# Sum of squares for 1/rms taken from the transposed input, with its row sent through memory

## The chip, the cores and the metric

The program runs on one core of a Trainium2 chip. The metric is the device time of one execution in microseconds (us); lower is better. The core has TensorE (PE in the profile; its weight loads are PEld), VectorE (DVE), ScalarE (ACT), GpSimd (POOL) and SyncE (SP), each with its own queue of instructions, and 16 DMA engines that move data between the chip's memory and the core's own memory. TensorE writes into PSUM banks; the other engines read them from there, except GpSimd, whose operands here are all in SBUF.

## The reference

The input is 512 tokens of 1024 features in FP32. One Mamba-2 layer comes first, then one projection to shared keys and values, then one layer of differential attention, and a last RMSNorm. The change lies in the first norm and the first product:

```
h = rms_norm(x, norm_g)          # y = x * rsqrt(mean(x*x, axis=-1) + EPS), then * g
zxbcdt = h @ w_in                # z (2048), x/B/C (4096), dt (32)
xbc = silu(conv(xbc)); dt = softplus(dt_raw + dt_bias)
y = ssd_chunked_scan(xs * dt, a * dt, bm, cm)   # decays exp(cumsum(a * dt))
y = gated_group_rms_norm(y + d_skip * xs, z, gate_norm_g)
x = x + y @ w_out
```

The norm's factor 1/rms is one number for each token. Since it multiplies a whole row of `h`, it can be applied after the product instead of before it.

## The kernel before

**Products.** Every FP32 operand is split into a high part (`hi`, rounded to fp32r) and the rest (`lo`), and each product is three fp32r products: hi*hi, hi*lo, lo*hi (`mm3`, `tok_mm`). The weights come in tiles of 1 MB (`raw`), in two buffers; ScalarE makes `whi` (with the norm's gain in it), VectorE `wlo`, in three buffers each. A tile serves 48 products of 512 columns. The transposed input `x_t` comes as four tiles `xt` of two feature blocks of 128 by 512 tokens; `split_x` makes `a_hi` and `a_lo` from them (named `hh` and `hl` in the code).

**The start.** TensorE first runs 17 transposes of the identity into a bank that nothing reads (`warm`). Then it runs the first half of the first z block (`pz0`: four token blocks by four feature blocks, 48 products) as the tiles come. ScalarE casts, VectorE subtracts; the two are held in program order there. The second half of z stands behind the setup of dt in the program, but it is not held there and runs ahead of it.

**1/rms.** The four token tiles `x_tok` are loaded behind the first weights; `squares` squares them on ScalarE with a sum along the features; `scales` takes the root on VectorE (`rsqrt`, a bit trick with two corrections), which gives `r_col`, 1/rms with the tokens on the partitions. For 1/rms along the free dimension on all partitions (`r_row`) GpSimd writes four diagonal blocks, TensorE multiplies a block of ones by them (`aps_r`, one FP32 product of 512 columns), and ScalarE copies the result. `r_col` scales the z block in `z_out` (Silu on ScalarE); `r_row` scales the dt rows and each x/B/C block in `conv`.

**dt and decays.** `ps_dt` is the dt product; `pre`, softplus and the running sum `acs` follow on VectorE and ScalarE. `acs` goes to memory and comes back broadcast to all partitions (`dec`) with two loads of 1 MB; its transposes (`ps_tt`, called "tt") give it by token. GpSimd subtracts and masks, ScalarE takes the exponential.

**Order.** A planner with a time simulation orders each engine's instructions; work that is ready may be put into an idle slot ahead of earlier work that is not. Where `T.on`, `A.on` or `V.on` is set, an instruction stays behind the one traced before it on its engine. From group 0 on TensorE's order is written out: `first_layer` counts one step for each three products, and `PLACES` says at which step after the end of each group's projection the parts of its scan run: "cb" the C*B product, "bt" and "xt" transposes, "st" the state products (`psA`, `psB`, `pyd`), "o1" and "o2" the outputs from the state, "y0" and "y2" the last transposes (`pyt`). "tt" is at step 22. TensorE waits where it reaches a part whose operands are late. The eight entries of a row are the groups 0 to 7.

**Queues.** Nearly all loads are issued by SP, in one order; a load that waits for a buffer holds back those behind it. The parameters `prm` go over ScalarE's queue.

Of the kernel before, what the change touches and what calls it, by code (L numbers as in the profile page):

```python
# [9 lines left out]
F32 = mybir.dt.float32  # L10
F32R = mybir.dt.float32r
I32 = mybir.dt.int32
AF = mybir.ActivationFunctionType
ALU = mybir.AluOpType
# [3 lines left out]
P = 128  # L18
S = 512
D = 1024  # L20
NT = S // P
# [17 lines left out]

PLACES = {  # L40
# [7 lines left out]
    "y2": (None,) * 7 + (72,),  # L48
}

# [28 lines left out]
def trunk(ctx, tc, x, x_t, par, w_dt, w_in, w_out, w_kvqg, w_bo, d_skip, lam_qk, fin_g, out):  # L79
# [16 lines left out]
    def ss_bank(name):  # L96
        turns[0] += 1
        tag = "mm" if turns[0] % turns[1] >= 3 else "ss"
        return psum.tile([P, 512], F32, tag=tag, name=name, bufs=3 if tag == "ss" else 4)

    def long_bank(name):
        return psum.tile([P, 512], F32, tag="long", name=name)
# [11 lines left out]
    nc.scalar.dma_start(prm[:], par[:, 0:C_CB])  # L114
    prc = const.tile([P, N_PAR - C_CB], F32, name="prc")
    x_tok = res.tile([P, NT, D], F32, name="x_tok")
    ident = const.tile([P, P], F32, name="ident")
    make_identity(nc, ident)
    sg1 = const.tile([P, 1], F32, name="sg1")
# [89 lines left out]
    def use(seg):  # L209
        fetch(segs.index(seg) + 3)  # L210
        return ready.pop(seg)
# [92 lines left out]
    def run(gen):  # L304
        for _ in gen:
            pass
# [13 lines left out]

    def squares(ss, t, sq=None):
        if sq is None:
            sq = small.tile([P, D], F32, tag="wide", name=f"sq{t}", bufs=2)
        A.activation(sq, x_tok[:, t, :], AF.Square, accum_out=ss[:, t:t + 1])

    def scales(tag, ss):

        V.tensor_scalar(out=ss, in0=ss, scalar1=ROOT2 / D, scalar2=ROOT2 * EPS, op0=ALU.mult, op1=ALU.add)  # L330
        col = const.tile([P, NT], F32, tag="r_col", name=f"{tag}r_col")
        V.tensor_copy(col, rsqrt(ss, NT, "y"))
        w = small.tile([P, NT + 1, P], F32, tag="wide", name=f"{tag}diag", bufs=2)
        GP.memset(w[:, NT], 1.0)
        for t in range(NT):
            GP.tensor_tensor(out=w[:, t], in0=ident, in1=col[:, t:t + 1].to_broadcast([P, P]), op=ALU.mult)
        ps = long_bank(f"{tag}ps_r")
        T.on = True
        T.matmul(ps, lhsT=w[:, NT], rhs=w[:, 0:NT].rearrange("p t n -> p (t n)"), start=True, stop=True)
        T.on = False  # L340
        row = res.tile([P, S], F32, tag="r_row", name=f"{tag}r_row")
        A.copy(row, ps)
        return col, row

    def turn_rows(tag, t, xn, hh, hl):

# [15 lines left out]
    def tok_mm(ps, t, b, w, ks=range(4)):  # L362
        tk = slice(t * P, (t + 1) * P)
        for k in ks:
            kk = 4 * b + k
            mm3(ps, (hh[:, kk, tk], hl[:, kk, tk]), (w[0][:, k, :], w[1][:, k, :]), b == 0 and k == 0, b == 1 and k == 3)
            yield
# [12 lines left out]
    def z_out(j, t, ps):  # L380

        for i in range(2):
            zs = bp2.tile([P, 256], F32, tag="zs", name=f"zs{j}_{t}_{i}", bufs=12)
            A.activation(zs, ps[:, i * 256:(i + 1) * 256], AF.Silu, scale=r_col[:, t:t + 1])
            zt[2 * j + i, t] = zs
# [1 line left out]


    warm = ss_bank("warm")
    for i in range(17):  # L390
        T.transpose(warm[:, 0:P], ident, ident)
    xt = [bp2.tile([P, 2, S], F32, tag="yl", name=f"xt{i}", bufs=4) for i in range(4)]

    def split_x(k, n=slice(0, S)):
        A.copy(hh[:, k, n], xt[k // 2][:, k % 2, n])
        V.tensor_tensor(out=hl[:, k, n], in0=xt[k // 2][:, k % 2, n], in1=hh[:, k, n].bitcast(F32), op=ALU.subtract)


# [4 lines left out]
    wh, wl = ready.pop(("z", 0, 0))  # L403
    pz0 = [mm_bank(f"pz0_{t}") for t in range(NT)]
    V.on = A.on = True
    for k in range(4):
        lay(first[k])
        for n in (slice(0, 256), slice(256, S)) if k < 2 else (slice(0, S),):
            split_x(k, n)
    V.on = A.on = False  # L410
    for k in range(4):
        for t in range(NT):
# [2 lines left out]
    for k in range(4, KD):  # L415
        split_x(k)
    fetch(2)
    for t in range(NT):
        nc.sync.dma_start(x_tok[:, t, :], x[t * P:(t + 1) * P, :])
    ss = bss[:, 1]  # L420
    for t in range(NT):
        squares(ss, t)
    r_col, r_row = scales("a", ss)
    V.tensor_scalar(out=sg1, in0=prm[:, C_SG:C_SG + 1], scalar1=0.5 * (1.0 - LAM0), scalar2=None, op0=ALU.mult)
    dtw_raw = sm.tile([P, KD, H], F32, name="dtw_raw")
    nc.sync.dma_start(dtw_raw[:], w_dt)
# [2 lines left out]


    V.tensor_tensor(out=dtw_raw, in0=dtw_raw, in1=prm[:, C_GA:C_GA + KD].unsqueeze(2).to_broadcast([P, KD, H]), op=ALU.mult)
    ps_dt = ss_bank("ps_dt")
    T.on = True
    for k in range(KD):
# [27 lines left out]
    A.activation(ea, prm[:, C_AL:C_AL + 1], AF.Exp)  # L462
    adt = q2
    V.tensor_scalar(out=adt, in0=dtp, scalar1=ea, scalar2=-1.0, op0=ALU.mult, op1=ALU.mult)
    ones = sm.tile([P, P], F32, name="ones")
    GP.memset(ones, 1.0)
    acs = e1
    V.tensor_tensor_scan(out=acs, data0=ones, data1=adt, initial=0.0, op0=ALU.mult, op1=ALU.add)
    acs_d = tc.dram_tile([H, NQ, P], F32, name="acs_d")
# [5 lines left out]
    nc.sync.dma_start(dsk[:], d_skip.partition_broadcast(P))  # L475


    w0 = use(("z", 0, 1))
    for t in range(NT):
        run(tok_mm(pz0[t], t, 1, w0))  # L480
        z_out(0, t, pz0[t])


    tok = const.tile([P, 4, NQ, H], F32, name="tok")
# [2 lines left out]
    def turned():  # L487
        yield "tt"
        ps_tt = ss_bank("ps_tt")
        for i, src in enumerate((dtp, acs, toe)):  # L490
            T.transpose(ps_tt[:, i * P:(i + 1) * P], src, ident)
        V.tensor_copy(tok[:, 0:3].rearrange("p a c h -> p (a c h)"), ps_tt[:, 0:3 * P])
        A.activation(tok[:, 3], tok[:, 1], AF.Exp)
        decays((0, 1))

    def runs_of(kind=1):

# [97 lines left out]
        assert not due  # L595

    decs = {}

    def decays(gs):

        for g in gs:
            hs = slice(R * g, R * g + R)
            both = bp.tile([P, N_DEC], F32, tag="dec", name=f"dec{g}", bufs=2)
            dec = both[:, 0:R * NQ * P].rearrange("p (h c l) -> p h c l", h=R, c=NQ)
            een = both[:, R * NQ * P:R * NQ * P + 2 * R].rearrange("p (h q) -> p h q", h=R)
            nc.sync.dma_start(both[:, 0:R * NQ * P],
                                acs_d[hs].rearrange("h c l -> (h c l)").partition_broadcast(P))
            GP.tensor_copy(een, dec[:, :, 1:3, P - 1])
            for h in range(R):
                GP.tensor_tensor(out=dec[:, h], in0=dec[:, h], in1=acs_tok[:, :, R * g + h].unsqueeze(2).to_broadcast([P, NQ, P]), op=ALU.subtract)  # L610
                GP.affine_select(out=dec[:, h], in_=dec[:, h], compare_op=ALU.is_ge, fill=-BIG, base=0,
                                 pattern=[[0, NQ], [1, P]], channel_multiplier=-1)
            decs[g] = (dec, een, both)

        for g in gs:
            A.activation(decs[g][2][:, 0:R * NQ * P + 2 * R], decs[g][2][:, 0:R * NQ * P + 2 * R], AF.Exp)
# [604 lines left out]
```

## Time and profile before

| | |
|---|---|
| median of 3 runs (lowest, highest) | 705.49 us (705.47, 708.14) |
| the profiled execution, whole | 707.18 us |
| its span in the profile | 705.4 us |
| mean granted TensorE clock | 0.998 |
| busy: PE, PEld, DVE, ACT, POOL | 696.1, 580.7, 524.2, 426.3, 116.1 us |
| moved by DMA | 70.85 MB |

The span runs from the first to the last instruction that the profile shows. Busy time is the time in which an engine has an instruction in work; the ends of matmuls are modelled, since they overlap, so the pace of TensorE is read from the starts of its instructions. In a row of the timeline stand the start and the length in us, the engine, the line (L70 is the helper through which VectorE, ScalarE and TensorE are called), the operation, output <- inputs, the shape, how many instructions are merged in the row, and in brackets the idle time before it and what ended it. A transpose is shown as a MATMUL, an FP32 product as two. A row of a group has the count, the busy time, the mean length in ns, and the idle time before.

### The profile page before, as it was taken

What the parts mean: (1) busy time and instruction counts of PE and PEld (TensorE: products, weight loads), DVE (VectorE), ACT (ScalarE), POOL (GpSimd) and SP (SyncE); (2) the same over time, 40 slices, a digit from 0 to 9 for tenths busy, and PEclk for the clock granted to TensorE, in tenths of its full rate; (3) what the DMA queues carried; (4) which work ended last, traced back from release to release, by engine and by line L of the source; (5) the groups of instructions that cost most, each with busy time, mean ns of one, the idle gap of its engine ahead of it and who ended that gap; (6) DMA issues with size and microseconds to landing.
All of it is one profiled execution on the core that took longest, in us unless ns stands there. A gap on an engine that the chain in (4) does not pass through costs nothing.

```text
span 705.4 us, 10468 instructions
## 1 busy us (share of the span) xinstructions
PE 696.1 (99%) x3838; PEld 580.7 (82%) x3838; DVE 524.2 (74%) x1181; ACT 426.3 (60%) x931; POOL 116.1 (16%) x158
## 2 busy tenths in 40 slices
PE   8999999999999999999999999999999999999996
PEld 7888788888878888888888888888888888888884
DVE  5499967799489679569995757557778757787776
ACT  6859663573654547536635258567777667665546
POOL 0008242502406025042110101000000000000002
PEclk9999999999999999999999999999999999999999
DMA  8654314214125323313222111513112221130103
GB/s 293 257 193 170 120 60 135 105 61 179 42 79 180 105 76 120 110 70 120 64 84 94 60 60 53 194 60 113 67 60 77 80 83 61 60 106 14 31 1 119
DMA packets 13491, 70.85 MB, mean 100 GB/s; under 512 B 1792, under 2 KB 3328, under 8 KB 6016
## 3 DMA queue, kind: packets, MB, share of 16 engines
q1 hardware_dynamic: 13008, 69.90, 27.6%
q8 instruction: 30, 0.49, 0.3%
q10 hardware_dynamic: 432, 0.28, 0.1%
q14 instruction: 21, 0.17, 0.1%
HBM read 68.02 MB, written 2.16 MB: 99 GB/s over the span
## 4 chain that ended last, share of the span: by engine, by line
PE 78%; DVE 8%; ACT 5%; DMA 4%; issue 3%; POOL 2%; SPq 0%; ACTq 0%; POOLq 0%; DVEq 0%
PE po L70 16%; PE pg L70 14%; PE pt L70 8%; PE pq L70 6%; PE pk L70 6%; PE pv L70 6%; PE pz L70 6%; PE pb L70 3%; DMA raw<-in_w_in 3%; PE sc L70 3%; DVE wlo L70 2%; ACT whi L70 2%; PE pc L70 2%; PE pyd L70 2%; DVE xc L70 1%
## 5 line engine op out<-in xcount | busy, mean ns | idle before, releaser
L70 DVE SCALAR_TENSOR_TENSOR wlo<-raw,prm,whi 128x512 fp32r<-128x512 f32 (+1 forms) x240 | 149.3, 672 | 54.0 <-ACT whi L70 53.7
L70 ACT ACTIVATE whi<-raw,prm 128x512 fp32r<-128x512 f32 (+1 forms) x240 | 133.2, 629 | 46.7 <-PE pg L70 12.0
L70 PE MATMUL pg<-a_hi,whi 128*128 128x512 f32 x256 | 102.8, 402 | 0.0
L70 PE MATMUL pg<-a_hi,wlo 128*128 128x512 f32 x256 | 99.9, 390 | 0.0
L70 PE MATMUL pg<-a_lo,whi 128*128 128x512 f32 x256 | 99.7, 389 | 0.0
L70 DVE SCALAR_TENSOR_TENSOR xc<-pg,prc,xc 128x511 f32<-128x511 f32 (+2 forms) x96 | 70.9, 743 | 12.3 <-ACT xc L70 11.2
L70 PEld LDWEIGHTS pg<-a_hi,wlo 128*128 128x128 f32 x256 | 48.1, 188 | 10.3
L70 PEld LDWEIGHTS pg<-a_hi,whi 128*128 128x128 f32 x256 | 48.2, 188 | 9.6 <-ACT zs L70 0.2
L70 PEld LDWEIGHTS pg<-a_lo,whi 128*128 128x128 f32 x256 | 48.1, 188 | 9.4
L70 PE MATMUL po<-whi,yh 128*128 128x512 f32 x128 | 51.2, 400 | 0.0
L70 PE MATMUL pz<-whi,a_hi 128*128 128x512 f32 x128 | 49.7, 397 | 0.3 <-ACT a_hi L70 0.3
L70 PE MATMUL po<-whi,yl 128*128 128x512 f32 x128 | 49.9, 390 | 0.0
L70 PE MATMUL po<-wlo,yh 128*128 128x512 f32 x128 | 49.9, 390 | 0.0
L70 PE MATMUL pz<-whi,a_lo 128*128 128x512 f32 x128 | 48.9, 390 | 0.0
L70 PE MATMUL pz<-wlo,a_hi 128*128 128x512 f32 x128 | 48.9, 389 | 0.0
L1026 POOL TENSOR_TENSOR ot<-x_tok,fg 128x512 f32<-128x512 f32 x4 | 5.0, 1284 | 246.8 <-DVE x_tok L70 246.8
L70 ACT ACTIVATE xc<-xc 128x512 f32<-128x512 f32 x32 | 20.2, 630 | 40.5 <-DVE xc L70 36.7
L70 ACT ACTIVATE xc<-pg,prc 128x512 f32<-128x512 f32 x32 | 24.8, 774 | 28.3 <-DVE pg L70 27.9
L70 DVE CUSTOM_DVE_ANT_0 s<-sc,bias 128x128 f32<-128x128 f32 (+3 forms) x64 | 29.4, 488 | 16.0 <-PE sc L70 15.5
L70 ACT ACTIVATE s<-s,mx 128x128 f32<-128x128 f32 (+3 forms) x64 | 35.6, 557 | 9.1 <-DVE mx L70 8.9
L651 POOL TENSOR_TENSOR xe<-xdt,tok 128x256 f32<-128x256 f32 x24 | 14.0, 613 | 159.3 <-DVE xdt L70 159.3
L70 ACT ACTIVATE tmp<-dx 128x256 f32<-128x256 f32 x32 | 13.1, 410 | 36.8 <-DVE dx L70 36.8
(237 smaller groups left out, 1651.1 us busy)
## 6 DMA issues: line engine op xcount, KB each, us to landing
raw<-in_w_in SPq DMA_DIRECT2D x22, 1024.0 KB, 4.9
raw<-in_w_kvqg SPq DMA_DIRECT2D x16, 1024.0 KB, 4.8
dec<-acs_d SPq DMA_DIRECT2D x8, 1024.0 KB, 5.1
raw<-in_w_out SPq DMA_DIRECT2D x8, 1024.0 KB, 4.9
raw<-in_w_bo SPq DMA_DIRECT2D x4, 1024.0 KB, 4.8
x_tok<-in_x SPq DMA_DIRECT2D x4, 512.0 KB, 9.0
out<-ot SPq DMA_DIRECT2D x6, 256.0 KB, 2.1
raw<-in_w_in SPq DMA_DIRECT2D x4, 256.0 KB, 4.9
```

Of the source, the lines that this page charges most:

```text
L70: i = op(*args, **kw)
L651: GP.tensor_tensor(out=xe[:, c], in0=xdt[:, c], in1=toe_tok[:, c, hs].unsqueeze(2).to_broadcast([P, R, HD]), op=ALU.mult)
L1026: GP.tensor_tensor(out=o, in0=y, in1=f, op=ALU.mult)
```

## The change

The sum of squares is taken from the four `xt` tiles that the first product needs anyway. ScalarE squares each (128 x 1024 elements), GpSimd adds the eight halves into `xsum` (128 x 512, seven adds), and four FP32 products with a column of ones sum over the partitions (`lay_sums`): each has a 128 x 128 block of `xsum` as its weights, one column as its moving side, and gives a token block's sums in one column. VectorE takes the root as before, with priority in the planner. `r_col` is written to memory over ScalarE's queue, transposed, and read back on SP, broadcast to all partitions, as `r_row`. The diagonals, `aps_r` and ScalarE's copy are gone.

The second half of the first z block now runs ahead of the dt product, held in order on TensorE: token block 0, the column products, token blocks 1 to 3, then `ps_dt`; the four `z_out` come after that in the program. `x_tok` is loaded behind the first two decay loads on SP. At the start VectorE casts the first 256 columns of the first feature block, which ScalarE did; and the 17 warming transposes become 10 FP32 products of a block of zeros, which VectorE clears, so that they don't need the identity. The block of ones is made earlier. Ten entries of `PLACES` are 1 to 3 steps later.

```
--- before.py
+++ after.py
@@ -39,12 +39,12 @@
 
 PLACES = {
     "cb": (10, 2, 14, 14, 5, 5, 14, 12),
-    "bt": (10, 29, 21, 44, 35, 25, 21, 37),
+    "bt": (10, 29, 21, 47, 35, 25, 23, 37),
     "xt": (18, 35, 31, 52, 43, 36, 31, 43),
-    "st": (27, 47, 37, 63, 53, 47, 38, 53),
-    "o1": (31, 47, 46, 63, 53, 47, 46, 53),
-    "o2": (31, 52, 46, 69, 60, 52, 46, 58),
-    "y0": (61, 85, 76, 99, 89, 85, 69, 69),
+    "st": (29, 47, 39, 63, 53, 47, 39, 53),
+    "o1": (34, 47, 46, 63, 53, 47, 46, 53),
+    "o2": (34, 52, 46, 69, 60, 52, 46, 58),
+    "y0": (61, 85, 79, 99, 89, 87, 69, 70),
     "y2": (None,) * 7 + (72,),
 }
 
@@ -114,6 +114,8 @@
     nc.scalar.dma_start(prm[:], par[:, 0:C_CB])
     prc = const.tile([P, N_PAR - C_CB], F32, name="prc")
     x_tok = res.tile([P, NT, D], F32, name="x_tok")
+    blank = small.tile([P, D], F32, tag="wide", name="blank", bufs=2)[:, 0:P]
+    V.memset(blank, 0.0)
     ident = const.tile([P, P], F32, name="ident")
     make_identity(nc, ident)
     sg1 = const.tile([P, 1], F32, name="sg1")
@@ -320,27 +322,20 @@
 
 
 
-    def squares(ss, t, sq=None):
-        if sq is None:
-            sq = small.tile([P, D], F32, tag="wide", name=f"sq{t}", bufs=2)
-        A.activation(sq, x_tok[:, t, :], AF.Square, accum_out=ss[:, t:t + 1])
-
-    def scales(tag, ss):
-
-        V.tensor_scalar(out=ss, in0=ss, scalar1=ROOT2 / D, scalar2=ROOT2 * EPS, op0=ALU.mult, op1=ALU.add)
-        col = const.tile([P, NT], F32, tag="r_col", name=f"{tag}r_col")
-        V.tensor_copy(col, rsqrt(ss, NT, "y"))
-        w = small.tile([P, NT + 1, P], F32, tag="wide", name=f"{tag}diag", bufs=2)
-        GP.memset(w[:, NT], 1.0)
+    def lay_sums():
+
+        pss = ss_bank("pss")
         for t in range(NT):
-            GP.tensor_tensor(out=w[:, t], in0=ident, in1=col[:, t:t + 1].to_broadcast([P, P]), op=ALU.mult)
-        ps = long_bank(f"{tag}ps_r")
-        T.on = True
-        T.matmul(ps, lhsT=w[:, NT], rhs=w[:, 0:NT].rearrange("p t n -> p (t n)"), start=True, stop=True)
-        T.on = False
-        row = res.tile([P, S], F32, tag="r_row", name=f"{tag}r_row")
-        A.copy(row, ps)
-        return col, row
+            T.matmul(pss[:, t:t + 1], lhsT=xsum[:, t * P:(t + 1) * P], rhs=ones[:, 0:1], start=True, stop=True)
+        ss = bss[:, 1]
+        with tc.high_priority():
+            V.tensor_scalar(out=ss, in0=pss[:, 0:NT], scalar1=ROOT2 / D, scalar2=ROOT2 * EPS, op0=ALU.mult, op1=ALU.add)
+            V.tensor_copy(r_col, rsqrt(ss, NT, "y"))
+        r_d = tc.dram_tile([NT, P], F32, name="r_d")
+        nc.scalar.dma_start(r_d.rearrange("t p -> p t"), r_col)
+        r_row = res.tile([P, S], F32, tag="r_row", name="r_row")
+        nc.sync.dma_start(r_row, r_d.rearrange("t p -> (t p)").partition_broadcast(P))
+        return r_row
 
     def turn_rows(tag, t, xn, hh, hl):
 
@@ -387,12 +382,13 @@
 
 
     warm = ss_bank("warm")
-    for i in range(17):
-        T.transpose(warm[:, 0:P], ident, ident)
+    for i in range(10):
+        T.matmul(warm[:, 0:P], lhsT=blank, rhs=blank, start=True, stop=True)
     xt = [bp2.tile([P, 2, S], F32, tag="yl", name=f"xt{i}", bufs=4) for i in range(4)]
 
-    def split_x(k, n=slice(0, S)):
-        A.copy(hh[:, k, n], xt[k // 2][:, k % 2, n])
+    def split_x(k, n=slice(0, S), laid=False):
+        if not laid:
+            A.copy(hh[:, k, n], xt[k // 2][:, k % 2, n])
         V.tensor_tensor(out=hl[:, k, n], in0=xt[k // 2][:, k % 2, n], in1=hh[:, k, n].bitcast(F32), op=ALU.subtract)
 
 
@@ -403,10 +399,11 @@
     wh, wl = ready.pop(("z", 0, 0))
     pz0 = [mm_bank(f"pz0_{t}") for t in range(NT)]
     V.on = A.on = True
+    V.tensor_copy(hh[:, 0, 0:256], xt[0][:, 0, 0:256])
     for k in range(4):
         lay(first[k])
         for n in (slice(0, 256), slice(256, S)) if k < 2 else (slice(0, S),):
-            split_x(k, n)
+            split_x(k, n, (k, n.start) == (0, 0))
     V.on = A.on = False
     for k in range(4):
         for t in range(NT):
@@ -415,12 +412,18 @@
     for k in range(4, KD):
         split_x(k)
     fetch(2)
-    for t in range(NT):
-        nc.sync.dma_start(x_tok[:, t, :], x[t * P:(t + 1) * P, :])
-    ss = bss[:, 1]
-    for t in range(NT):
-        squares(ss, t)
-    r_col, r_row = scales("a", ss)
+    xsum = res.tile([P, S], F32, tag="r_row", name="xsum")
+    ones = sm.tile([P, P], F32, name="ones")
+    GP.memset(ones, 1.0)
+    for i in range(4):
+        sq = small.tile([P, 2, S], F32, tag="wide", name=f"sq{i}", bufs=2)
+        A.activation(sq, xt[i], AF.Square)
+        if i:
+            GP.tensor_tensor(out=xsum, in0=xsum, in1=sq[:, 0], op=ALU.add)
+            GP.tensor_tensor(out=xsum, in0=xsum, in1=sq[:, 1], op=ALU.add)
+        else:
+            GP.tensor_tensor(out=xsum, in0=sq[:, 0], in1=sq[:, 1], op=ALU.add)
+    r_col = const.tile([P, NT], F32, name="r_col")
     V.tensor_scalar(out=sg1, in0=prm[:, C_SG:C_SG + 1], scalar1=0.5 * (1.0 - LAM0), scalar2=None, op0=ALU.mult)
     dtw_raw = sm.tile([P, KD, H], F32, name="dtw_raw")
     nc.sync.dma_start(dtw_raw[:], w_dt)
@@ -429,6 +432,15 @@
 
 
     V.tensor_tensor(out=dtw_raw, in0=dtw_raw, in1=prm[:, C_GA:C_GA + KD].unsqueeze(2).to_broadcast([P, KD, H]), op=ALU.mult)
+    w0 = use(("z", 0, 1))
+    T.on = True
+    for t in range(NT):
+        run(tok_mm(pz0[t], t, 1, w0))
+        if t == 0:
+            r_row = lay_sums()
+    T.on = False
+    for t in range(NT):
+        z_out(0, t, pz0[t])
     ps_dt = ss_bank("ps_dt")
     T.on = True
     for k in range(KD):
@@ -462,8 +474,6 @@
     A.activation(ea, prm[:, C_AL:C_AL + 1], AF.Exp)
     adt = q2
     V.tensor_scalar(out=adt, in0=dtp, scalar1=ea, scalar2=-1.0, op0=ALU.mult, op1=ALU.mult)
-    ones = sm.tile([P, P], F32, name="ones")
-    GP.memset(ones, 1.0)
     acs = e1
     V.tensor_tensor_scan(out=acs, data0=ones, data1=adt, initial=0.0, op0=ALU.mult, op1=ALU.add)
     acs_d = tc.dram_tile([H, NQ, P], F32, name="acs_d")
@@ -475,10 +485,6 @@
     nc.sync.dma_start(dsk[:], d_skip.partition_broadcast(P))
 
 
-    w0 = use(("z", 0, 1))
-    for t in range(NT):
-        run(tok_mm(pz0[t], t, 1, w0))
-        z_out(0, t, pz0[t])
 
 
     tok = const.tile([P, 4, NQ, H], F32, name="tok")
@@ -492,6 +498,9 @@
         V.tensor_copy(tok[:, 0:3].rearrange("p a c h -> p (a c h)"), ps_tt[:, 0:3 * P])
         A.activation(tok[:, 3], tok[:, 1], AF.Exp)
         decays((0, 1))
+        with tc.issue_after(last_dec[0].ins):
+            for t in range(NT):
+                nc.sync.dma_start(x_tok[:, t, :], x[t * P:(t + 1) * P, :])
 
     def runs_of(kind=1):
 
@@ -595,6 +604,7 @@
         assert not due
 
     decs = {}
+    last_dec = [None]
 
     def decays(gs):
 
@@ -603,8 +613,8 @@
             both = bp.tile([P, N_DEC], F32, tag="dec", name=f"dec{g}", bufs=2)
             dec = both[:, 0:R * NQ * P].rearrange("p (h c l) -> p h c l", h=R, c=NQ)
             een = both[:, R * NQ * P:R * NQ * P + 2 * R].rearrange("p (h q) -> p h q", h=R)
-            nc.sync.dma_start(both[:, 0:R * NQ * P],
-                                acs_d[hs].rearrange("h c l -> (h c l)").partition_broadcast(P))
+            last_dec[0] = nc.sync.dma_start(both[:, 0:R * NQ * P],
+                                            acs_d[hs].rearrange("h c l -> (h c l)").partition_broadcast(P))
             GP.tensor_copy(een, dec[:, :, 1:3, P - 1])
             for h in range(R):
                 GP.tensor_tensor(out=dec[:, h], in0=dec[:, h], in1=acs_tok[:, :, R * g + h].unsqueeze(2).to_broadcast([P, NQ, P]), op=ALU.subtract)
```

## The prediction

> **What bounds the kernel now.** I read the page's first table, then TensorE's timeline, then those of ScalarE, VectorE and GpSimd over the first 50 us, then the DMA issues. From the page, the span and the busy shares:
>
> ```profile
> span 705.4 us, 10468 instructions
> PE 696.1 (99%) x3838; PEld 580.7 (82%) x3838; DVE 524.2 (74%) x1181; ACT 426.3 (60%) x931; POOL 116.1 (16%) x158
> ```
>
> TensorE is busy all the time, so only three things can change the time: when its stream starts, what is in it, and where it stands still. TensorE's timeline, start and length first, at the places that the change touches, and the same kind of work undisturbed beside them (149 against 195 us, 162 against 73 us):
>
> ```profile
> 1.47 3.89 PE L70 MATMUL warm<-ident 128*128 128x128 f32 x17 [1.47 <-POOL ident masks.py:199]
> 5.71 1.43 PE L70 MATMUL pz<-whi,a_hi 128*128 128x512 f32 x4 [0.35 <-ACT a_hi L70]
> 6.98 1.08 PE L70 MATMUL pz<-wlo,a_hi 128*128 128x512 f32 x4
> ...
> 9.72 1.07 PE L70 MATMUL pz<-wlo,a_hi 128*128 128x512 f32 x4
> ...
> 27.86 1.02 PE L70 MATMUL aps_r<-adiag 128*128 128x512 f32 x2
> 28.80 1.95 PE L70 MATMUL ps_dt<-xt,dtw_raw 128*32 128x128 f32 x64
> 30.69 0.50 PE L70 MATMUL pg<-a_hi,whi 128*128 128x512 f32 x1
> ...
> 45.80 0.27 PE L70 MATMUL ps_tt<-ident,pre 128*128 128x128 f32 x1
> ...
> 60.08 1.05 PE L70 MATMUL pcb<-xc,xc 128*128 128x128 f32 x8
> 60.97 0.49 PE L70 MATMUL pbt<-ident,xc 128*128 128x128 f32 x3
> 61.21 0.48 PE L70 MATMUL pg<-a_hi,whi 128*128 128x512 f32 x1
> ...
> 73.56 0.39 PE L70 MATMUL pg<-a_hi,wlo 128*128 128x512 f32 x1
> 74.39 1.27 PE L70 MATMUL psA<-xe,bt 128*128 128x256 f32 x4 [0.45 <-POOL xe L651]
> ...
> 78.18 0.50 PE L70 MATMUL pg<-a_hi,whi 128*128 128x512 f32 x1
> ...
> 149.69 1.03 PE L70 MATMUL pyt<-ident,tmp 128*128 128x128 f32 x8
> ...
> 150.81 0.48 PE L70 MATMUL pg<-a_hi,whi 128*128 128x512 f32 x1
> ...
> 162.70 1.02 PE L70 MATMUL psA<-xe,bt 128*128 128x256 f32 x4
> ...
> 166.10 0.50 PE L70 MATMUL pz<-whi,a_hi 128*128 128x512 f32 x1
> ...
> 194.97 0.49 PE L70 MATMUL pbt<-ident,xc 128*128 128x128 f32 x3
> ...
> 197.52 0.47 PE L70 MATMUL pg<-a_hi,whi 128*128 128x512 f32 x1
> ```
>
> Twelve products lie between 6.98 and 9.72: one each 0.228 us. The first four took 1.27 us (5.71 to 6.98) where 0.91 is normal: 0.36 lost. From 73.79 (73.56 and one product) to 78.18 are 4.39 us, the same work at 162 us takes 3.40: 0.99 lost in group 0. The eight `pyt` and three `pbt` transposes take 1.12 us at 149.69 and 2.55 at 194.97: 1.43 lost in group 2.
>
> **Part 1, operands sooner.** ScalarE's and VectorE's timeline, start and length first:
>
> ```profile
> 4.54 0.72 ACT L70 ACTIVATE whi<-raw,prm 128x512 fp32r<-128x512 f32 x1 [1.86 <-DMA prm<-in_par]
> 5.27 0.69 ACT L70 CAST a_hi<-xt 128x256 fp32r<-128x256 f32 x2
> 8.69 0.73 ACT L70 ACTIVATE whi<-raw,prm 128x512 fp32r<-128x512 f32 x1 [0.51 <-DMA raw<-in_w_in]
> 10.47 0.72 ACT L70 ACTIVATE whi<-raw,prm 128x512 fp32r<-128x512 f32 x1 [0.53 <-DMA raw<-in_w_in]
> 12.43 1.14 ACT L70 CAST a_hi<-xt 128x512 fp32r<-128x512 f32 x2 [0.68 <-DMA xt<-in_x_t]
> 16.38 1.34 ACT L70 ACTIVATE whi<-raw,prm 128x512 fp32r<-128x512 f32 x2 [0.15 <-DMA raw<-in_w_in]
> 17.14 1.41 DVE L70 SCALAR_TENSOR_TENSOR wlo<-raw,prm,whi 128x512 fp32r<-128x512 f32 x2
> 17.87 1.06 ACT L70 ACTIVATE sq<-x_tok 128x1024 f32<-128x1024 f32 x1 [0.15 <-DMA x_tok<-in_x]
> 18.84 0.18 ACT L70 ACTIVATION_READ_ACCUMULATOR sq<-x_tok 128x1 f32 x1
> ```
>
> ```profile
> 1.17 0.90 SPq L179 DMA_DIRECT2D xt<-in_x_t  x2
> ```
>
> ```profile
> xt<-in_x_t SPq DMA_DIRECT2D x2, 128.0 KB, 3.5
> ```
>
> The first product now waits for `whi` (4.54 to 5.26) and after it for the cast of 256 columns on the same engine. VectorE takes over that cast. Its input is issued at 1.17 and lands 3.5 us later (the DMA issues up to 2.1 us), at 4.7; the cast is about 0.4, from ScalarE's two in 0.69. So the first product goes at 5.31, 0.40 sooner; ScalarE's second half is there by 5.7, so the 0.36 goes too if it was that wait. I take 0.76; bounds 0 (the landing is later than `whi`'s end) and 0.76. The ten warming products start sooner, after a memset in place of the mask's two steps. By `pcb`'s four FP32 products in 0.89 us (60.08 to 60.97) ten take 2.2 us, at half pace 4.5; they end before 5.3 and cost nothing.
>
> **Part 2, the sum of squares.** Removed: four loads of `x_tok` ahead of the weights, four squares, the diagonals and `aps_r`. Added: four squares of `xt`, seven GpSimd adds, four column products behind the first token block's second half. TensorE's order is fixed there, so while the sum isn't ready everything behind waits: three token blocks, `ps_dt`, group 0. When does TensorE arrive? After 48 and 12 products: 5.31 + 60 x 0.2275 = 18.96. When is the sum ready? ScalarE stood idle 0.51, 0.53, 0.68 and 0.15 us between 8.2 and 16.4, together 1.87, and finished the weights at 17.72. Four squares at 0.97 (17.87 to 18.84) are 3.88, so weights and squares end at 17.72 + 3.88 - 1.87 = 19.7 at the earliest. GpSimd's groups, with mean length:
>
> ```profile
> L610 POOL TENSOR_TENSOR dec<-dec,tok 128x512 f32<-128x512 f32 x32 | 34.7, 1112 | 0.6
> L1026 POOL TENSOR_TENSOR ot<-x_tok,fg 128x512 f32<-128x512 f32 x4 | 5.0, 1284 | 246.8 <-DVE x_tok L70 246.8
> ```
>
> An add of that width is 1.11 to 1.28. If a square is last, two adds follow: 19.7 + 2.2 = 21.95, and the column products start at 22.0: a new wait of 3.05. If the weights are last, `wlo` (0.7) and two products follow: about 21.05, a wait of 2.1. If two squares come behind the weights, four adds of 1.28 follow from 18.7: 23.8, a wait of 4.9. I take 3.05: a square has the lower priority, so it tends to be last.
>
> The four column products replace `aps_r` (27.86 to 28.80, 0.94). Their weights are as large as those of `pcb`'s four in 0.89, their moving side is one column; the lower bound is `pbt`'s 0.08 each (60.97 to 61.21), 0.3 in all. I take 0.8, nearest to `pcb`: a gain of 0.14 (0.05 to 0.64).
>
> The row through memory: 1/rms takes 2.2 us after the sums, as now:
>
> ```profile
> 22.97 0.17 DVE L70 TENSOR_SCALAR bss<-bss 128x4 f32<-128x4 f32 x1 [0.47 <-ACT sq L70]
> ...
> 24.96 0.17 DVE L70 COPY ar_col<-y_y 128x4 f32<-128x4 f32 x1
> 35.57 1.19 DVE L70 TENSOR_TENSOR pre<-ps_dt,ar_row 32x128 f32<-32x128 f32 x4 [0.29 <-ACT ar_row L70]
> ```
>
> ```profile
> prm<-in_par ACTq DMA_DIRECT2D x1, 21.5 KB, 3.8
> dec<-acs_d SPq DMA_DIRECT2D x8, 1024.0 KB, 5.1
> ```
>
> The column is there at 22.8 + 2.2 = 25.0. A write as long as `prm`'s 3.8, a read at most `dec`'s 5.1 and two issues of 0.4 make 34.7. It is needed when `pre` may start: TensorE reaches `ps_tt` 15.1 us after group 0 starts (30.69 to 45.80), and the dt chain takes 10.2 from `pre` to there (35.57 to 45.80). Group 0 would start at 22.8 + 36 x 0.2275 + 1.89 (`ps_dt`, 28.80 to 30.69) = 32.9, `ps_tt` at 48.0, so the row may come at 37.8. It costs nothing with 3.1 us to spare; behind the waiting issue on SP stand weights two tiles ahead. The Trainium skill, in "DMA: Bandwidth & Descriptors", "Rules for kernel authors", speaks against this write: a strided last dimension is lowered to one descriptor per element, here 512 of four bytes. No row shows such a write; by the rule alone the sum stays, and the rival below gets its chance.
>
> **Part 3, moved.** `x_tok`'s four loads (2 MB) go behind the first decay loads, past later weights on SP. Their first reader is the first output projection, five stages on; weights behind them come at most 10.2 us later, by twice `dec`'s 5.1 for 1 MB, and one weight tile lasts 48 products, 10.9 us, with two loaded ahead. Nothing, or up to 1 us if that cover is thin. The places: a step of one is three products, 0.68 us. Group 0's `st` goes back two (1.37, over the 0.99 lost), group 2's `y0` three (2.05, over the 1.43). I take both whole: 2.42; bounds 0 and 2.42, as the work that was late could come later too. The other places show no such loss, so nothing.
>
> **The sum**, against the profiled execution (707.18, span 705.4): -0.76 + 3.05 - 0.14 - 2.42 = -0.27, so 706.9; the median of the runs stands 1.69 below, 705.49, so 705.2. With the ends of the wait alone: 704.3 to 707.1.
>
> **Rivals.** (a) No new wait: the squares lie early enough. For it: the sum has idle ScalarE slots from 8.2 on; against it: 1.87 us of idle don't hold 3.88. 705.49 - 0.76 - 0.14 - 2.42 = 702.2. (b) TensorE's pace falls after the wait. At the start 17 transposes took 3.89 us, 0.23 each, against 0.08 at 60.97, though products ran at full pace by 6.98; a slow stretch of that length (3.4 to 5.5 us) at half pace costs 1.7 to 2.7: 705.2 + 2.2 = 707.4. It decides at some idle length above the 0.45 seen at 74.39, which had no slow work behind it. The Trainium skill, in "TensorE: Matmul & The Clock Gate", Part 1, says that an idle window of about 3.4 us halves the clock; by that rule a wait of 3.05 costs nothing and one of 4.9 may. (c) The slower one: the row is late. If 512 pieces cost four times `prm`'s 128, the write is 15.2 us, not 3.8; it decides at 3.8 + 3.1 = 6.9, and `ps_tt` then stops TensorE for 15.2 - 6.9 = 8.3: 713.5. For it, only the piece count; against it, pieces run on 16 engines at once. (d) The place moves give nothing, since the late work moves with TensorE: 705.2 + 2.4 = 707.6.
>
> **How the numbers follow.** Forecast 0.50, (a) 0.22, (b) 0.06, (c) 0.05, (d) 0.17. The range reaches from (a) with the column products at their cheapest (702.2 - 0.5 = 701.7) to (d) with the 1 us of the later loads on top (708.6): 701.6 to 708.6. The likeliest's own is 704.3 to 707.1. No change is within 0.5%, about what a measurement of this kernel can tell: 702.0 to 709.0. Faster holds the lower part of (a), 0.10; slower (c) and the top of (b) and (d), 0.08; the rest, 0.82, is no change.
>
> **What would show it.** The first `pz` product at 5.3 instead of 5.71; an idle of TensorE before the column products, released by GpSimd, of 2 to 5 us, with group 0 starting near 32.9; `psA` in 3.4 us and `pyt` of group 2 with `pbt` in 1.12; no wait at `ps_tt`. The prediction is wrong if the column products have no wait, if `ps_tt` waits for a chain that starts with the row, or if the losses at 74 and 195 us return elsewhere.

## The result and the profile after

The changed kernel takes 723.97 us (median of 6 runs, 723.08 to 725.07), the kernel before 706.02 (705.47 to 708.14): ratio 1.0247, 95% interval 1.0229 to 1.0266. It is slower; the prediction of 705.2 and its range of 701.6 to 708.6 were wrong. The profiled execution took 724.03 us, 16.9 more than that of before.

The page of the changed kernel, its span, busy times and granted clock in 40 slices:

```profile
span 722.2 us, 10495 instructions
PE 702.8 (97%) x3847; PEld 586.6 (81%) x3847; DVE 529.1 (73%) x1183; ACT 425.0 (59%) x925; POOL 125.0 (17%) x160
PEclk9798999999999999999999999999999999999999
```

TensorE has lost its 99%, and its clock is down in the second and fourth slice (18 to 36 and 54 to 72 us). TensorE's longest waits from 10 to 70 us, summed by line (total, times, longest), say what for; in the kernel before that stretch had none:

```profile
PE ps_tt L70 <- DVE pre L70: 5.7, 1, 5.7
PE pz L70 <- DVE wlo L70: 5.6, 3, 3.4
```

Neither is the wait that the prediction counted: nothing waits for GpSimd. TensorE's timeline shows where they lie:

```profile
5.83 1.34 PE L70 MATMUL pz<-whi,a_hi 128*128 128x512 f32 x4
7.00 1.08 PE L70 MATMUL pz<-wlo,a_hi 128*128 128x512 f32 x4
...
18.83 0.50 PE L70 MATMUL pz<-wlo,a_hi 128*128 128x512 f32 x1 [1.44 <-DVE wlo L70]
...
20.53 0.50 PE L70 MATMUL pz<-wlo,a_hi 128*128 128x512 f32 x1 [0.73 <-DVE wlo L70]
...
24.90 0.79 PE L70 MATMUL pz<-wlo,a_hi 128*128 128x512 f32 x1 [3.41 <-DVE wlo L70]
...
27.20 1.70 PE L70 MATMUL pss<-ones,xsum 128*128 128x1 f32 x8
28.76 0.77 PE L70 MATMUL pz<-whi,a_hi 128*128 128x512 f32 x1
29.33 0.63 PE L70 MATMUL pz<-wlo,a_hi 128*128 128x512 f32 x1
29.76 0.63 PE L70 MATMUL pz<-whi,a_lo 128*128 128x512 f32 x1
...
41.19 0.50 PE L70 MATMUL pg<-a_hi,whi 128*128 128x512 f32 x1
...
56.05 0.39 PE L70 MATMUL pg<-a_hi,wlo 128*128 128x512 f32 x1
62.12 0.48 PE L70 MATMUL ps_tt<-ident,pre 128*128 128x128 f32 x1 [5.68 <-DVE pre L70]
...
63.53 0.78 PE L70 MATMUL pg<-a_hi,whi 128*128 128x512 f32 x1
...
67.52 0.43 PE L70 MATMUL pg<-a_hi,whi 128*128 128x512 f32 x1
...
94.19 1.02 PE L70 MATMUL psA<-xe,bt 128*128 128x256 f32 x4
...
97.59 0.50 PE L70 MATMUL pg<-a_hi,whi 128*128 128x512 f32 x1
...
215.02 0.49 PE L70 MATMUL pbt<-ident,xc 128*128 128x128 f32 x3
215.35 1.04 PE L70 MATMUL pyt<-ident,tmp 128*128 128x128 f32 x8
216.14 0.48 PE L70 MATMUL pg<-a_hi,whi 128*128 128x512 f32 x1
```

- **Before group 0**: it starts at 41.19 instead of 30.69, 10.50 later. Three waits for `wlo` cost 6.07 beyond the normal 0.23 per product (1.60 + 0.90 + 3.57, from the start of the product ahead of each to its own). From 24.90 products go one each 0.43 us (29.33 to 29.76) until 33.2: this costs 1.2 on the five ahead of `pss` and 2.3 on the 36 behind it, and `pss` takes 1.56, not the 0.94 of `aps_r`: 0.6 more. Together 10.2.
- **At `ps_tt`**: 56.05 and a product to 63.53 are 7.25 us, against 0.55 before (45.80 to the next product): 6.70 lost; nine products behind it at half pace lose 2.0 more (63.53 to 67.52).
- **The places** worked: `psA` to the next product 3.40 (94.19 to 97.59) instead of 4.39, `pbt` and `pyt` of group 2 take 1.12 (215.02 to 216.14), where 2.55 were taken before: 0.99 and 1.43 gained, 2.42 as counted.

10.50 + 6.70 + 2.0 - 2.4 = 16.8, the difference of the two spans (722.2 and 705.4).

Why `wlo` is late: VectorE's and GpSimd's timelines of the changed kernel over that stretch.

```profile
13.95 3.15 DVE L70 TENSOR_TENSOR a_lo<-xt,a_hi 128x512 fp32r<-128x512 f32 x2 [0.67 <-ACT a_hi L70]
17.02 3.46 DVE L70 SCALAR_TENSOR_TENSOR wlo<-raw,prm,whi 128x512 fp32r<-128x512 f32 x2
20.40 3.45 DVE L70 TENSOR_TENSOR a_lo<-xt,a_hi 128x512 fp32r<-128x512 f32 x2
```

```profile
13.55 1.29 POOL L422 TENSOR_TENSOR xsum<-xsum,sq 128x512 f32<-128x512 f32 x1 [3.26 <-ACT sq L70]
...
21.70 1.60 POOL L423 TENSOR_TENSOR xsum<-xsum,sq 128x512 f32<-128x512 f32 x1
```

A pair of `wlo` takes 3.46 us, where the prediction's row (17.14) has 1.41; a pair of `a_lo` takes 3.15 and 3.45, where 1.29 was normal (13.08 in the trace of before). Nearly all of it lies beside the adds. The adds end at 23.3, and `pss` starts at 27.20: the sum was never what TensorE waited for.

Why `pre` is late: the write and the read of the row in the chain of work that ended last (start and length).

```profile
35.50 11.83 DMA r_d<-r_col
...
47.47 5.92 DMA r_row<-r_d
```

The write of 2 KB in 512 pieces of 4 bytes takes 11.9 us (from 35.50 until SP's read of it is released at 47.36), the read 5.9; the row is there at 53.4. The column itself comes at 35.5, not 25.0: `pss` is late, and the 1/rms chain took 6.5 us instead of 2.2, since `wlo` pieces lie between its steps on VectorE (one of these waited 1.07 us for ScalarE's `whi`, with the chain's next step behind it).

### The profile page after: what moved, and what is told of

It reads as the page before. It is cut to its first block, busy times and chain, and to the rows that moved or that the text cites. A ratio compares the mean times of both kernels' runs of the same rounds, so it can differ in the third digit from the quotient of the medians.

```text
span 722.2 us, 10495 instructions
## 1 busy us (share of the span) xinstructions
PE 702.8 (97%) x3847; PEld 586.6 (81%) x3847; DVE 529.1 (73%) x1183; ACT 425.0 (59%) x925; POOL 125.0 (17%) x160
## 4 chain that ended last, share of the span: by engine, by line
PE 89%; DMA 5%; DVE 3%; issue 1%; ACT 1%; ACTq 0%; SPq 0%; DVEq 0%
PE pg L70 22%; PE po L70 16%; PE pz L70 9%; PE pt L70 7%; PE pq L70 6%; PE pk L70 6%; PE pv L70 6%; PE pb L70 3%; PE sc L70 3%; PE pyd L70 2%; PE pc L70 2%; DMA r_d<-r_col 2%; DMA raw<-in_w_in 2%; PE pyt L70 1%; PE pcb L70 1%
## 5 line engine op out<-in xcount | busy, mean ns | idle before, releaser
L70 DVE SCALAR_TENSOR_TENSOR wlo<-raw,prm,whi 128x512 fp32r<-128x512 f32 (+1 forms) x240 | 151.8, 682 | 53.7 <-ACT whi L70 53.6
```

Of the source, the lines that this page charges most:

```text
L70: i = op(*args, **kw)
```

## The experiments

Two theories of the first loss stood against each other: **A**, GpSimd's adds slow VectorE while they run; **B**, ScalarE's four squares stand ahead of the weights and make `whi`, and so `wlo`, late. Of the second: the write of the row is slow by its pieces, or the row is late because the column is.

**Six of the seven adds left out.** Only the last tile's two halves are added, so the sum is too small; everything else is there.

```
-        if i:
-            GP.tensor_tensor(out=xsum, in0=xsum, in1=sq[:, 0], op=ALU.add)
-            GP.tensor_tensor(out=xsum, in0=xsum, in1=sq[:, 1], op=ALU.add)
-        else:
+        if i == 3:
             GP.tensor_tensor(out=xsum, in0=sq[:, 0], in1=sq[:, 1], op=ALU.add)
```

> The changed kernel with six of the seven GpSimd adds left out (only the last squares are added, so the sum is too small); the squares stay. Theory A, GpSimd's adds slow VectorE down while both run: VectorE's a_lo of 512 columns is back at 0.69 us from 1.5 and wlo at 0.75 from 1.77, TensorE's waits for wlo before group 0 fall from 6.1 us to under 1.5, the stretch at half pace behind them is gone, and group 0 starts 7 to 9 us sooner than at 41.19. The row from memory is then late by more, so the whole time falls by less, to 714 to 719 us. Theory B, ScalarE's squares push the weights back and VectorE is late for that: the waits stay at 4 to 6 us and the time within 2 us of 724.

718.52 us, ratio 1.0181 (1.0165 to 1.0197). VectorE's timeline and TensorE's waits from 10 to 70 us:

```profile
16.02 1.41 DVE L70 SCALAR_TENSOR_TENSOR wlo<-raw,prm,whi 128x512 fp32r<-128x512 f32 x2 [0.80 <-ACT whi L70]
```

```profile
PE ps_tt L70 <- DVE pre L70: 8.8, 1, 8.8
PE pz L70 <- DVE wlo L70: 1.0, 1, 1.0
PE pz L70 <- ACT whi L70: 0.7, 1, 0.7
```

`wlo` and `a_lo` are back at 0.7 each; the waits ahead of group 0 fall to 1.7 and there is no half pace there: group 0 starts at 33.0. A holds; about 2.3 us remain, with the squares (B). Of the 8.2 us that group 0 gains, 3.1 go straight into the wait at `ps_tt`, which ends with the row.

**The squares left out**, the adds reading the inputs themselves (so the sum is not one of squares):

```
-        sq = small.tile([P, 2, S], F32, tag="wide", name=f"sq{i}", bufs=2)
-        A.activation(sq, xt[i], AF.Square)
+        sq = xt[i]
```

> The changed kernel with ScalarE's four squares left out; GpSimd adds the inputs themselves, so the sum is of x and not of its squares. Theory A (GpSimd slows VectorE): a_lo stays near 1.5 us while the adds run, TensorE waits 3 to 6 us for wlo, and the time stays at 719 to 724 us. Theory B (the squares push the weights back): the waits fall under 1 us and group 0 starts 8 us sooner, though the adds still run.

722.04 us, ratio 1.023 (1.0216 to 1.0244). `a_lo` and `wlo` still take 1.5 to 1.8 each while the adds run, and ahead of group 0 TensorE waits for them in five pieces of at most 1.2 us; none is followed by half pace. Group 0 starts at 37.56. So against the kernel before (30.69) the adds without the squares cost 6.9 us there, 1.4 of them a wait for `zs`, and the squares without the adds 2.3; together they cost 10.5. The split is not clean, since without the squares the adds also run earlier (7.85 to 19.0 instead of 9.0 to 23.3). B alone doesn't explain the loss's main part. At `ps_tt` TensorE then waits 7.5 us.

**Six adds replaced by memsets** of the same kind of tile, four per tile: GpSimd writes, and reads nothing.

```
-            GP.tensor_tensor(out=xsum, in0=xsum, in1=sq[:, 0], op=ALU.add)
-            GP.tensor_tensor(out=xsum, in0=xsum, in1=sq[:, 1], op=ALU.add)
...
+        if i < 3:
+            for _ in range(2):
+                GP.memset(sq[:, 0], 0.0)
+                GP.memset(sq[:, 1], 0.0)
```

> The changed kernel with six of the seven GpSimd adds replaced by memsets of the same squares (four of 128x512 for each of the first three tiles), so GpSimd is busy at the same time but only writes; the sum is too small. If what slows VectorE is that both read two operands from SBUF, VectorE's a_lo stays at 0.69 us and wlo at 0.75 beside the memsets, and the kernel runs as the one without adds, 718.5 us within 1.5. If GpSimd's being busy is enough, a_lo is over 1.0 us and the waits for wlo are over 4 us. The Trainium skill, in "SBUF - State Buffer", "Who interferes with whom", says that a VectorE instruction with two SBUF inputs contends with a GpSimd one that reads SBUF and not with one that only writes it; by it the first comes out.

719.1 us, ratio 1.0198 (1.0177 to 1.0219), near the kernel without adds. VectorE's and GpSimd's timelines:

```profile
15.51 1.41 DVE L70 SCALAR_TENSOR_TENSOR wlo<-raw,prm,whi 128x512 fp32r<-128x512 f32 x2 [0.80 <-ACT whi L70]
```

```profile
15.86 0.53 POOL L423 MEMSET sq<- 128x512 f32 x1
```

Beside a GpSimd that only writes, VectorE keeps its pace (1.41 for the pair); beside one that reads it takes 2.4 times as long (3.46). The Trainium skill, in "SBUF — State Buffer", "Who interferes with whom", says just this: an instruction of VectorE with two inputs in SBUF meets a GpSimd instruction that reads SBUF, not one that only writes it. The traces agree.

**The row without memory**, from diagonals and one product behind `ps_dt`:

```
+            GP.tensor_tensor(out=w[:, t], in0=ident, in1=r_col[:, t:t + 1].to_broadcast([P, P]), op=ALU.mult)
...
+        T.matmul(ps, lhsT=ones, rhs=w.rearrange("p t n -> p (t n)"), start=True, stop=True)
+        A.copy(r_row, ps)
```

> The changed kernel with the row of 1/rms made as before, by diagonals on GpSimd and one product of 512 columns behind the dt product, without the way through memory. If the write and the read of the row are what the dt chain waits for, TensorE's 5.7 us before ps_tt and the 2 us at half pace behind it are gone: 715 to 717 us. If the late 1/rms column (35.5 us) is enough to make it late, 2 us or more of the wait stay: 719 us or more.

715.85 us, ratio 1.0144 (1.013 to 1.0158). TensorE's waits from 10 to 70 us:

```profile
PE pz L70 <- DVE wlo L70: 6.1, 3, 3.1
```

The wait at `ps_tt` and the half pace behind it are gone, the first loss stays.

**The row in 128 pieces of 16 bytes.** It still goes through memory; its tokens stand in another order.

```
-        nc.scalar.dma_start(r_d.rearrange("t p -> p t"), r_col)
+        nc.scalar.dma_start(r_d.rearrange("t (q a) -> (t q) a", a=NT), r_col)
```

> The changed kernel with 1/rms written to memory as 128 pieces of 16 bytes in place of 512 pieces of 4; the tokens of the row come out in another order, so the result is another one. If the 11.9 us of the write go with the number of pieces, the write takes 3 to 5 us, TensorE's 5.7 us before ps_tt and the half pace behind it go, and the time is 715 to 717 us. If a write to memory takes that long whatever its pieces, the write stays at 10 us or more and the time at 723 to 725 us.

714.8 us, ratio 1.0129 (1.0115 to 1.0143). The DMA issues and TensorE's timeline:

```profile
r_row<-r_d SPq DMA_DIRECT2D x1, 256.0 KB, 3.1
r_d<-r_col ACTq DMA_DIRECT2D x1, 2.0 KB, 5.5
```

```profile
55.81 0.27 PE L70 MATMUL ps_tt<-ident,pre 128*128 128x128 f32 x1
```

The same bytes in a quarter of the pieces take 5.5 us instead of 11.9, and the column, as late as before, is then early enough: no wait. So it is the pieces that make the row late here. 9.2 us come back: the two terms in the trace (6.70 + 2.0), and 0.5 by which group 0 starts sooner in this trace. The rule of the Trainium skill on a strided last dimension ("DMA: Bandwidth & Descriptors", "Rules for kernel authors"), which the prediction cited, was the one to price.

**Both halves**, adds left out and the row without memory:

> Six of the seven GpSimd adds left out (so the sum of squares lacks six of its eight tiles' halves, and 1/rms is wrong) and the row made from diagonals and one product instead of through memory. If the loss of the changed kernel is GpSimd's slowing of VectorE plus the late row and nothing else, both halves add up: group 0 starts 2.3 us later than in the kernel before (33.0, as without the adds), ps_tt doesn't wait, no half pace, the places give 2.4 back: 706.0, ratio 1.000 within 0.003. If the two losses overlapped or a third cause is there (the loads' new places, the start, the half pace by another way), it stays above 709.

708.31 us, ratio 1.0031 (1.0015 to 1.0047), just above the 1.003 at which the expectation ended. By the medians 15.7 of the 18 us lost are these two causes. `ps_tt` comes at 47.81 in its trace, 2.0 later than before: one wait of 1.0 for `wlo` stays, behind the squares. The places' gain stands against that, and its profiled execution, the shortest of twelve, took 706.5; so what the last 2 us of the median are, the trace doesn't show.

**Products in the gap ahead of `ps_tt`**, six FP32 ones of 512 columns:

```
+        for i in range(6):
+            T.matmul(pf, lhsT=ident, rhs=xt[3][:, 1, :], start=True, stop=True)
```

> The changed kernel with six FP32 products of 512 columns ahead of the ps_tt transposes, into a bank that nothing reads: 5.6 us of work where TensorE now waits 5.7 us. If TensorE's pace halves because it stood idle, the nine products at 0.43 us behind ps_tt run at 0.23 and the time is 1.5 to 2.5 us less, 722 us. If the half pace has another cause (the FP32 transposes, or group 0's late operands), it stays and the time is that of the changed kernel, 724, or more.

731.6 us, ratio 1.0367 (1.0353 to 1.0381). TensorE's timeline behind the gap, and its waits from 10 to 100 us:

```profile
62.99 0.39 PE L70 MATMUL pg<-a_lo,whi 128*128 128x512 f32 x1
63.22 0.39 PE L70 MATMUL pg<-a_hi,wlo 128*128 128x512 f32 x1
```

```profile
PE pxt L70 <- ACT xc L70: 6.9, 2, 5.5
```

Behind `ps_tt` products go one each 0.23 us at once: with TensorE busy in the gap, there is no half pace. The total was missed: new waits of 6.9 us for `xc` came later, with half pace again behind the one of 5.5. Why `xc` is late with the added products stays open.

**The places alone**, in the kernel before:

> The kernel before with the new PLACES alone. If the losses at 74 us (0.99) and 195 us (1.43) go as the changed kernel's trace shows it, 2.4 us less than before, 703.6 us. If there they went only since TensorE ran later, the late work moves along and the time is that of before within 0.5 us.

705.85 us, ratio 0.9995 (0.9982 to 1.0008): no change. In group 0, where the changed kernel took 1.1 us for `pbt` and `pyt`, this one loses 0.9 (its TensorE timeline):

```profile
103.13 1.93 PE L70 MATMUL pyt<-ident,tmp 128*128 128x128 f32 x8
```

**The places with `y0` of group 0 at 63** instead of 61:

> The kernel before with the new places alone, and y0 of group 0 at 63 instead of 61. With 61 the eight pyt transposes there took 1.93 us instead of 1.03, waiting for ScalarE's tmp, which ended at 104.25. If they were only too early, two steps (1.37 us) more give that 0.9 back: span 703.1, median 705.0, ratio 0.9985. If the late work moves with TensorE, the 0.9 us is lost at the new place or behind it, and the median stays at 705.8.

705.67 us, ratio 0.9987 (0.9976 to 0.9998): about 0.1% faster than the kernel before, hardly more than the uncertainty. Inside its trace groups 0 and 2 give 2.46 together, measured between the same products as in the trace of before; 1.4 us were lost earlier: the second group of four products went 0.44 later than in the trace of before, and `aps_r` waited 1.04 for GpSimd's diagonals.

**The sooner start alone**, in the kernel before:

> The kernel before with the start of the changed one alone: VectorE's cast of the first 256 columns, and ten warming products of zeros. If the cast is what the first product waited for, it starts 0.4 us sooner and the time is 705.6 against 706.0. If the start is set by the parameters' landing and by TensorE's slow pace in its first us, the second group of four products starts no sooner than at 6.7 to 7.0, and the time is that of before within 0.3.

709.64 us, ratio 1.0058 (1.0045 to 1.007): 3.9 us slower, though in the trace the first product goes at 5.29 and the second group of four at 6.34. That row, and TensorE's waits from 10 to 60 us:

```profile
6.34 1.07 PE L70 MATMUL pz<-wlo,a_hi 128*128 128x512 f32 x4
```

```profile
PE aps_r L70 <- POOL adiag L338: 1.5, 1, 1.5
PE ps_tt L70 <- DVE e L70: 1.1, 1, 1.1
PE ps_tt L70 <- DVE pre L70: 0.8, 1, 0.8
```

GpSimd's four diagonals, 1.47 us in the kernel before, took 2.82 beside VectorE's `wlo` (26.05 to 28.87). Two kernels moved them, to ScalarE (`A.activation(w[:, t], ident, AF.Copy, scale=col[:, t:t + 1])`) and to VectorE (`V.tensor_scalar(out=w[:, t], in0=ident, scalar1=col[:, t:t + 1], scalar2=None, op0=ALU.mult)`), both with the sooner start:

> The kernel before with the sooner start alone, and the four diagonals by ScalarE instead of GpSimd. With GpSimd they took 2.82 us instead of 1.47 (26.05 to 28.87), beside VectorE's four wlo, and TensorE waited 1.52 us for them and then 1.9 at ps_tt. If that meeting of the two engines is the cause of the loss of 3.9 us, the wait at aps_r goes and the kernel is at 705.3 (0.4 to 0.64 sooner): ratio 0.9995. If the start itself delays the chain (the column is there 0.76 us later, the weights' loads lag 0.9), the wait at ps_tt stays at about 1 us or more and it is at 707 to 709.

> The kernel before with the sooner start alone and the four diagonals by VectorE. If the meeting of GpSimd's diagonals with VectorE's wlo is the first cause of what the start lost (709.64), aps_r doesn't wait for them (1.52 and 1.22 in the two kernels tried) and 1.5 to 2 of 3.9 us come back: 707.5 to 708. If ps_tt's wait goes too, it was late by the same cause: 705.5. If ps_tt still waits 1.9 and the median is over 708.5, the loss at ps_tt is a cause of its own: VectorE's order there, with wlo pieces ahead of the chain's last steps.

On ScalarE 711.03 us, ratio 1.0063 (1.0047 to 1.0079): the diagonals lie behind four `whi`, and `aps_r` still waits 1.2; at `ps_tt` TensorE waits 0.36, 2.25 and 0.45. On VectorE 710.57 us, ratio 1.006 (1.0039 to 1.0081): four in 0.87 us, no wait at `aps_r`, and the loss is at `ps_tt` now. Its longest TensorE wait and VectorE's timeline:

```profile
PE ps_tt L70 <- DVE pre L70: 2.4, 1, 2.4
```

```profile
43.18 1.93 DVE L70 SCALAR_TENSOR_TENSOR pl<-pl,q 128x128 f32<-128x128 f32 x6
45.02 0.75 DVE L70 SCALAR_TENSOR_TENSOR wlo<-raw,prm,whi 128x512 fp32r<-128x512 f32 x1
...
46.76 1.41 DVE L70 SCALAR_TENSOR_TENSOR wlo<-raw,prm,whi 128x512 fp32r<-128x512 f32 x2
48.08 0.28 DVE L70 SCALAR_TENSOR_TENSOR pre<-pre,pl 128x128 f32<-128x128 f32 x1
```

In the kernel before the eight `pl` steps and `pre` run without a break, 42.01 to 44.91, and the `wlo` come behind; here four `wlo` lie between them (one of them behind the dots), in the same order as in the kernel with the start alone. Behind `ps_tt` products then go at half pace for some 3 us in both kernels, which the profiled execution of the start alone doesn't show. So the meeting of the diagonals with `wlo` costs the wait at `aps_r`, but the larger loss is at `ps_tt`, behind another order on VectorE. That this order is its cause is read from the traces; no kernel put the order back. What in the start edit turns it stays open.

**The places, `y0` at 63, and the diagonals on VectorE**, without the start:

> The kernel before with the new places (y0 of group 0 at 63) and the four diagonals by VectorE right behind the column, instead of by GpSimd. With GpSimd they met VectorE's wlo when the loads came 1.3 us later (2.82 us instead of 1.47, and a wait of 1.04 at aps_r in that execution). If that meeting costs the runs of that kernel their gain, aps_r doesn't wait, and the median falls from 705.7 to 704.6, ratio 0.9975. If the diagonals only push wlo back as far as they were late themselves, it stays at 705.7 (0.9987).

705.5 us, ratio 0.9985 (0.9971 to 0.9999): no better than with the diagonals on GpSimd (0.9987), though its trace has no wait at `aps_r`. These two come out ahead of the kernel before, by about 0.1%.

## Why the prediction was wrong

- **Part 2, the sum of squares (+3.05 counted)**. This is the step that failed. It priced the seven adds on GpSimd alone and asked when the sum is ready; it never asked what else the adds slow. The waits came ahead of the column products and for `wlo`: 6.07 us, and with the half pace behind them 10.2. When the sum was ready didn't decide: the adds, at 1.6 each against the 1.28 taken, end at 23.3, four us ahead of the column products. The trace of before held the warning: later, beside GpSimd's `dec` work, a pair of `wlo` takes longer than the 1.42 it has at 14.42, in VectorE's timeline of before:

```profile
57.38 1.97 DVE L70 SCALAR_TENSOR_TENSOR wlo<-raw,prm,whi 128x512 fp32r<-128x512 f32 x2
```

- **The row through memory (nothing counted, 3.1 us to spare)**. Failed twice. The write, priced as `prm`'s 3.8, took 11.9; rival (c) had named the mechanism and its price (15.2) and gave it 0.05. Its argument against, that pieces run on 16 engines at once, proved no bound. That the loss at `ps_tt` (6.70 + 2.0) is near the 8.3 that rival (c) gave is in part luck: its write was 3.3 too long, and it had no half pace. The column came 10.5 us later than the 25.0 counted and group 0 8.3 later than 32.9, which by itself didn't decide: with the write in 128 pieces the row was in time.
- **Rival (b), TensorE's pace**. It happened twice, behind the third wait for `wlo` (3.5 us, and 0.6 in `pss`) and behind `ps_tt` (2.0); the prediction gave it 0.06 at the price of 2.2. The mechanism was right, and the price fits the second time but is half of the first. It looked for a length of one wait at which the pace falls; the last section shows that shorter waits do it too when they lie close together.
- **The swap of `aps_r` for the column products (-0.14)**. At full pace `pss` takes 0.81 us (in the kernels without adds, without squares and with memsets), as counted; in the changed kernel it met the half pace and took 1.56.
- **Part 1, operands sooner (-0.76)**. In the changed kernel nothing was gained: the second group of four stands at 7.00 instead of 6.98, since `prm` landed at 5.05 there instead of 4.54. With the start alone it came 0.64 sooner in the trace, in the two kernels that also move the diagonals only 0.10 and 0.16 (6.88, 6.82); the waits at `aps_r` and `ps_tt` turned the gain into a loss of 3.9. A gain at the head of the stream was counted as if the stream behind stayed as it was.
- **Part 3, the places (-2.42)**. Right to 0.01 inside the trace of the changed kernel. Alone they changed nothing in the medians, which is rival (d)'s result; in the trace 0.9 is lost anew at group 0's `y0`, and with `y0` at 63 they gave 0.1%. Part 3 took its losses from an execution 1.2 us above its kernel's median (707.18 and 706.02); whether the others have them whole, no trace shows. The loads of `x_tok` cost nothing that the trace shows.

Two of the prediction's own signs of being wrong came: the column products had no wait of their own, and `ps_tt` waited for a chain that starts with the row. The sum of the parts rested on one kind of price: each operation's length in a trace where it stood alone. Both large errors are prices of operations in company or in another shape.

## What to carry to other kernels

Before work is moved to GpSimd, list what VectorE does in that stretch: if VectorE's instructions there have two inputs in SBUF and GpSimd's read SBUF, price VectorE's at twice their length or more (here 2.4), and look in the trace for a place where the two already meet. A transfer of small pieces is priced by its pieces as well as its bytes (here 2 KB took 11.9 us in 512 pieces and 5.5 in 128); where the nearest row has fewer, larger pieces, its time is a lower bound only. When a stream that is 99% busy gains waits, add them up over a few us, add what the slower pace behind them costs, and look past the wait for whoever was timed to arrive with it.

## What was not expected of the hardware

- VectorE's six 128x512 instructions from 13.95 on in the changed kernel, each with two inputs, took 1.45 to 1.78 us beside GpSimd's adds instead of 0.69 to 0.75, so about as long as an add (1.60 to 1.62, against 1.29 where it began alone). The two engines go in step: the last five of these start 0.39 or 0.40 us behind the start of an add (14.92 and 15.32 to 21.70 and 22.10).
- TensorE's pace falls and comes back at the borders of fixed windows of 3.41 us. The stretches at half clock last 10.24 us (23.2 to 33.4) and 6.83 (60.75 to 67.6) in the changed kernel, 13.65 with the row without memory, 3.41 with the diagonals on ScalarE: whole multiples. The changed kernel in a view by such windows (length; busy time and count of TensorE, its weight loads, VectorE, ScalarE, GpSimd; granted clock, DMA share, GB/s):

```profile
16.38:19.79 3.41, 1.97 (x8) 0.99 (x6) 3.41 (x3) 3.41 (x6) 3.25 (x3) 1.00 0.65 271
19.79:23.21 3.42, 0.97 (x4) 0.49 (x3) 3.42 (x3) 2.60 (x5) 3.26 (x3) 1.00 0.01 2
23.21:26.62 3.41, 1.72 (x4) 1.43 (x5) 3.41 (x6) 0.01 (x1) 0.09 (x1) 0.50 0.12 19
26.62:30.03 3.41, 3.41 (x13) 3.02 (x13) 1.31 (x5) 0.00 (x0) 0.00 (x0) 0.50 0.74 286
30.03:33.45 3.42, 3.42 (x9) 2.65 (x9) 2.21 (x9) 1.78 (x3) 0.00 (x0) 0.50 0.53 160
```

  In all fifteen traces the clock halves behind each such window in which TensorE was busy 1.46 us or less and behind none with 1.70 or more. So no length of a single wait decides: with the row without memory the pace fell at 21.6, behind waits of 2.28 and 0.73 with products between them (1.41 busy in that window); in the kernel with 128 pieces the same two waits fell across a border (1.70 and 1.92 busy) and it didn't, until the third wait. The full pace came back behind windows with 3.23 us busy or more and not behind 3.05 or less; four windows that look full but hold the column products `pss`, as 26.62 to 30.03, didn't bring it back.

  The Trainium skill, in "TensorE: Matmul & The Clock Gate", Part 1, gives an idle window of about 3.4 us for the halving and a busy one of that length for the way back. The length agrees (3.41); the window need not be idle, since up to 1.46 us of work in it didn't keep the clock up.
- A write of 512 pieces of 4 bytes took 10.1 to 11.9 us in the traces, of 128 pieces of 16 bytes 5.5; the read of the row behind it took 4.8 to 6.5 and 3.1.
